# The head of a decoder trunk loaded by row group, contiguous weight chunks, and a changed TensorE ranking in the planner

## The chip, the cores and the metric

The kernel runs on one core of a Trainium2 chip (trn2). The metric is the device time of one execution in microseconds; a lower number is better. Three runs of the kernel before gave 301.43, 301.76 and 303.13 us, with a median of 301.76.

## The reference

Two layers act on x of 256 tokens by 1024 features, in float32. Each layer does the following, and a final RMSNorm comes after the second.

```python
def hybrid_layer(x, norm_w, w_in, conv_w, conv_b, gate_bias, ret_norm_w, mlstm_norm_w, w_out):
    h = rmsnorm(x, norm_w)
    proj = jnp.matmul(h, w_in)           # 1024 x 4360, all groups at once
    (aq, ak, av, ag, bq, bk, bv, bg, cq, ck, cv, co, cg, ci, cf) = jnp.split(proj, cuts, axis=-1)
    ya = moba_attention(aq, ak, av) * silu(ag)                    # 8 heads of 64, ALiBi, causal
    yb = head_norm(retention(rotate(bq), rotate(bk), bv)) * silu(bg)   # 4 heads of 64
    qk = silu(causal_dwconv(concat(cq, ck), conv_w, conv_b))
    yc = head_norm(mlstm(qk, cv, ci, cf) * sigmoid(co)) * silu(cg)     # 4 heads of 64
    return x + jnp.matmul(concat(ya, yb, yc), w_out)              # 1024 x 1024
```

At 256 tokens the attention sees one block, so it is plain causal softmax with a linear bias.

## The kernel before

**Numbers.** Each float32 operand of a projection is split into a high part (rounded to fp32r) and a low part (the rest), and a product is three matmuls: high x high, high x low, low x high. ScalarE writes the high part (`A(h, raw, Copy)`), VectorE the low part (`V("tensor_tensor", lo, raw, h, subtract)`). So every weight passes ScalarE and VectorE once.

**Chunks.** The weights of a layer lie in chunks of about 1 MB: `aq0`, `ak0`, `bq`, `bk`, `cq`, `ck`, `cvif` and so on, then four chunks of `w_out`. A chunk has 128 partitions; its columns run over 8 row groups (`k`, 128 input features each). `loader` fetches chunk after chunk into the pool `raw` (3 buffers), `splitter` writes `hi` and `lo` (3 buffers each), `project` issues the matmuls, and functions named `evac_...` take the results from PSUM and go on with attention, retention and mLSTM (`head_a`, `head_c`, `pair_a` and others).

**The head.** The first two chunks, `aq0` and `ak0`, are projected together, row group by row group: for each `k`, two chunks `z`, two column halves `t`, and three products, so 12 matmuls of 256 columns. `loader` fetches for the row groups 0, 1, 2-3, 4-5 and 6-7 one transfer of x and one of each chunk: 15 transfers. `first_x` splits x of a group (it also multiplies by the norm's weight), `first_w` the weights. In DRAM x lies as `[128, 80 + 8*256]` with the small parameters in front (`xp`), and all weights as one array `w` of `[128, 2*43072]`, so that a row of a chunk is 344,576 bytes from the next.

**Order.** One order for each engine's queue is written out beforehand by a planner, class `Sched`. Every piece of work is a generator (a thread with a priority) that yields operations with an engine and a cost in ns: `V` for VectorE, `A` for ScalarE, `G` for GpSimd, `M` and `TR` for TensorE matmuls and transposes, `D` for a DMA on SP's queue. `Sched.run` takes again and again the operation that could start first by its model (`start`, then the priority, then the age) and emits it. `LAT` (230 ns) is what it reckons for a hand-over to another engine, 1100 ns for a landing. `pause(t)` delays a thread's next operation to a time of the model; it stands before the transposes of `norm` and of `head_a`. The order is fixed once the kernel is built; at run time the engines wait for each other's semaphores only. `project` has priority 5, the attention parts 2, so these go first where both could start.

**Warm-up.** Two float32 matmuls on a zeroed tile (`dummy`, L372) precede the work on TensorE.

Almost all instructions are recorded under the lines of the helpers: L259 is `V`, L265 `A`, L280 `M`, L285 `TR`, L288 `D`. A tile's name tells more than a line: `xx` is the split x, `hi` and `lo` the split weights, `px` parameters and x, `pj` and `mx` the PSUM banks, `st`, `zu`, `zd` the split operands of the heads, `t` the pool `t512`, `et` the weights of the heads' values.

## Time and profile before

| | |
|---|---|
| Profiled execution, its time | 301.41 us |
| Its span, first to last instruction | 299.6 us |
| Median of the runs | 301.76 us |
| TensorE busy | 291.0 us, 97% |
| VectorE busy | 257.7 us, 86% |
| ScalarE busy | 196.6 us, 66% |
| GpSimd busy | 15.3 us, 5% |
| DMA | 48.58 MB, 162 GB/s over the span |
| Granted TensorE clock | 0.995 |

The profile is one execution. Busy shares are averages over very different stretches: a head in which data arrive, two layers, and an end in which the last rows are normed and written. TensorE's matmuls are pipelined: the duration of one overlaps the next, so the distance from start to start tells what a matmul costs in a stream. In a row of the timeline stand start, duration, engine, line, operation, output and input, shape, count, and in brackets the idle time before with what ended it. In a row of groups, busy time and the mean duration of one in ns follow the bar.

### The profile page before, as it was taken

How to read it: one execution, taken by the hardware profiler on the slowest of the kernel's cores; microseconds unless marked ns; L12 is line 12 of the kernel's file. 1: busy time of each engine (PE TensorE's matmuls, PEld its weight loads, DVE VectorE, ACT ScalarE, POOL GpSimd, SP SyncE). 2: the span in 40 equal slices, each digit the busy share in tenths (PEclk: the TensorE clock that was granted, in tenths of full speed). 3: DMA queues.
4: the chain of work that ended last, by engine and by line, in shares of the span. 5: the costliest groups of instructions: out<-in, count | busy, mean ns of one | idle time of the engine just before them, and what ended most of it. 6: DMA issues, size and time to landing. Idle time of an engine off the chain costs nothing.

```text
span 299.6 us, 4795 instructions
## 1 busy us (share of the span) xinstructions
PE 291.0 (97%) x1792; PEld 258.2 (86%) x1792; DVE 257.7 (86%) x549; ACT 196.6 (66%) x341; POOL 15.3 (5%) x19
## 2 busy tenths in 40 slices
PE   8899999999999999999999999999999999999991
PEld 6798989888989888899988898988899988888881
DVE  3969999999999997985679999999999999956353
ACT  5958997889448539644666699779555265845332
POOL 6000000000002002000020000000002002000010
PEclk9999999999999999999999999999999999999997
DMA  6999456574710560754317663446541624330003
GB/s 200 374 398 352 153 174 223 184 258 143 238 45 0 161 240 22 249 174 148 136 19 264 205 222 125 156 142 219 203 142 45 237 67 173 123 131 0 2 0 140
DMA packets 9095, 48.58 MB, mean 162 GB/s; under 512 B 1008, under 2 KB 1904, under 8 KB 4080
## 3 DMA queue, kind: packets, MB, share of 16 engines
q1 hardware_dynamic: 9072, 48.28, 46.7%
q8 instruction: 14, 0.23, 0.3%
q14 instruction: 9, 0.07, 0.1%
HBM read 47.23 MB, written 1.05 MB: 161 GB/s over the span
## 4 chain that ended last, share of the span: by engine, by line
PE 91%; DVE 2%; issue 2%; ACT 1%; DMA 1%; SPq 1%; POOL 0%; POOLq 0%
PE pj L280 71%; PE mx L280 15%; PE mx L285 4%; DMA px<-xp 1%; SPq L288 1%; DVE sb L259 1%; DVE t L259 1%; ACT t L265 0%; ACT hi L265 0%; POOL small L554 0%; ACT xx L265 0%; ACT raw L265 0%; POOLq L1207 0%; DVE raw L259 0%; DVE hc L259 0%
## 5 line engine op out<-in xcount | busy, mean ns | idle before, releaser
L259 DVE TENSOR_TENSOR lo<-raw,hi 128x1024 fp32r<-128x1024 f32 (+2 forms) x96 | 102.8, 1087 | 8.9 <-ACT hi L265 8.7
L265 ACT ACTIVATE hi<-raw 128x1024 fp32r<-128x1024 f32 (+2 forms) x96 | 88.8, 946 | 10.4 <-DMA raw<-w 4.6
L280 PE MATMUL pj<-hi,xx 128*128 128x512 f32 (+1 forms) x320 | 94.4, 374 | 0.0
L280 PE MATMUL pj<-xx,hi 128*128 128x512 f32 (+1 forms) x272 | 88.0, 377 | 0.7 <-ACT hi L265 0.7
L280 PE MATMUL pj<-xx,lo 128*128 128x256 f32 x240 | 68.8, 287 | 0.3 <-DVE lo L259 0.3
L280 PEld LDWEIGHTS pj<-hi,xx 128*128 128x128 f32 x320 | 57.4, 188 | 9.0
L280 PE MATMUL pj<-lo,xx 128*128 128x512 f32 (+1 forms) x160 | 59.4, 371 | 0.0
L280 PEld LDWEIGHTS pj<-xx,hi 128*128 128x128 f32 x272 | 49.9, 192 | 10.1 <-ACT hi L265 1.7
L280 PEld LDWEIGHTS pj<-xx,lo 128*128 128x128 f32 x240 | 45.8, 191 | 0.8 <-DVE lo L259 0.7
L280 PEld LDWEIGHTS pj<-lo,xx 128*128 128x128 f32 x160 | 30.1, 188 | 4.5
L265 ACT ACTIVATE sb<-sb,small 128x128 f32<-128x128 f32 (+1 forms) x48 | 19.5, 448 | 4.9 <-DVE small L259 2.4
L265 ACT ACTIVATE t<-pj 128x256 f32<-128x256 f32 x26 | 9.8, 376 | 17.0 <-PE pj L280 16.9
L265 ACT ACTIVATE st<-t 64x512 fp32r<-64x512 f32 x26 | 16.1, 627 | 4.5 <-DVE t L259 4.2
L1101 POOL TENSOR_TENSOR small<-small,mhalf 128x8 f32<-128x8 f32 x4 | 6.9, 1731 | 181.7 <-DVE small L259 181.7
L280 PE MATMUL pj<-yh,lo 128*128 128x256 f32 x56 | 15.9, 284 | 0.0
L280 PE MATMUL pj<-yh,hi 128*128 128x256 f32 x56 | 15.9, 284 | 0.0
L280 PE MATMUL pj<-yl,hi 128*128 128x256 f32 x56 | 15.8, 283 | 0.0
L280 PE MATMUL mx<-st,st 128*128 128x128 f32 (+1 forms) x64 | 15.1, 270 | 0.0
L265 ACT ACTIVATE t<-pj,small 128x512 f32<-128x512 f32 (+1 forms) x12 | 7.3, 610 | 11.2 <-PE pj L280 11.2
L259 DVE TENSOR_TENSOR t<-pj,t 128x256 f32<-128x256 f32 x26 | 10.9, 419 | 2.2 <-ACT t L265 2.1
L265 ACT ACTIVATE t<-t 32x512 f32<-32x512 f32 (+1 forms) x20 | 12.6, 629 | 0.3
L280 PEld LDWEIGHTS mx<-st,st 128*128 128x128 f32 x64 | 12.1, 189 | 0.6
(150 smaller groups left out, 480.3 us busy)
## 6 DMA issues: line engine op xcount, KB each, us to landing
raw<-w SPq DMA_DIRECT2D x37, 1024.0 KB, 4.8
raw<-w SPq DMA_DIRECT2D x2, 1056.0 KB, 6.2
raw<-w SPq DMA_DIRECT2D x6, 256.0 KB, 5.6
raw<-w SPq DMA_DIRECT2D x2, 512.0 KB, 6.8
tb<-tab SPq DMA_DIRECT2D x1, 960.0 KB, 10.0
px<-xp SPq DMA_DIRECT2D x3, 256.0 KB, 4.8
tb<-tab SPq DMA_DIRECT2D x1, 514.0 KB, 7.7
raw<-w SPq DMA_DIRECT2D x4, 128.0 KB, 2.8
```

The lines of the kernel that those rows point to most:

```text
L259: return op("dve", cost, lambda: getattr(nc.vector, name)(out, *a, **k), after)
L265: return op("act", cost, lambda: nc.scalar.activation(out, in_, func, **k), after)
L280: return op("pe", cost, lambda: nc.tensor.matmul(out, a, b, start=start, stop=stop, skip_group_check=True), after)
L285: return op("pe", 110.0, lambda: nc.tensor.transpose(out, in_, idn))
L288: return op("sp", cost, lambda: nc.sync.dma_start(out, in_))
L1101: yield G(1600, lambda: nc.gpsimd.tensor_tensor(vs, vs, mhalf[:, :8], op=OP.pow))
```

## The change

- **Head in DRAM and SBUF.** x and the first two chunks are interleaved by row group in one array `hd` and one tile `px`: for each `k` 256 columns of x, 256 of `aq0`, 256 of `ak0` (`H_K` = 768). Groups 0 and 1 come as three transfers each, groups 2 to 7 as one each: 12 transfers. Each transfer's block is contiguous in DRAM. The head no longer takes buffers of the pool `raw`.
- **Chunks.** Each later chunk is contiguous in DRAM (`block`).
- **Splitting the head.** For groups 2 to 7 both chunks are split in one step of 512 columns. The very first weight is rounded on VectorE. The first six matmuls go by product before column half, and wait for each operand by itself.
- **Buffers.** `on_a`, `on_b`, `hc` and four of the six `t512` buffers lie in places of `px` whose weights have been split.
- **Start.** Seven 128-column matmuls on a constant zero replace the two on a zeroed tile. `va`, `vc` and `cpad` are set only where nothing else writes.
- **Planner.** Matmul costs are 120.2 ns for 256 columns (before 110) and 226.8 for 512 (before 216.3). A TensorE operation that follows another engine, or has waited, is ranked as if it could start 400 ns later (`SLACK`); the time that the model then books for it is unchanged. Both `pause` calls are gone.

The diff, cut to its core:

```diff
--- before
+++ after
@@ -53,8 +53,11 @@
 W_OFFS = np.concatenate([[0], np.cumsum(W_SIZES)]).tolist()
+W_HEAD = W_OFFS[2]
 W_TOTAL = W_OFFS[-1]
+H_K = 256 + 512
@@ -114,6 +117,8 @@
+    SLACK = 400.0
     SELF = {"pe": 0.0, "dve": 130.0, "act": 130.0, "pool": 130.0, "sp": 0.0}
@@ -200,14 +205,16 @@
                         ready = max(ready, th.floor)
-                    start = max(self.free.get(eng, 0.0), ready)
+                    free = self.free.get(eng, 0.0)
+                    start = max(free, ready)
+                    by = max(free, ready + self.SLACK) if eng == "pe" and (th.src != "pe" or th.floor > th.t) else start
                     if alt is None or start + cost < alt[0]:
-                        alt = (start + cost, start, way)
+                        alt = (start + cost, start, way, by)
                 prio = th.prio() if callable(th.prio) else th.prio
-                key = (alt[1], prio, th.seq)
+                key = (alt[3], prio, th.seq)
                 if best is None or key < best[0]:
-                    best = (key, th, alt[2])
-            (start, _, _), th, (eng, cost, fn, after) = best
+                    best = (key, th, alt[2], alt[1])
+            _, th, (eng, cost, fn, after), start = best
             self.live.remove(th)
@@ -226,7 +233,7 @@
 @with_exitstack
-def trunk(ctx: ExitStack, tc: tile.TileContext, xp: bass.AP, w: bass.AP, fn: bass.AP,
+def trunk(ctx: ExitStack, tc: tile.TileContext, hd: bass.AP, w: bass.AP, fn: bass.AP,
           tab: bass.AP, out: bass.AP):
@@ -274,9 +281,9 @@
         if a.dtype == F32R:
-            cost = max(107.0, n / 2.4) + 3
+            cost = max(113.0, n / 2.4 + 13.5)
         else:
-            cost = 2 * max(107.0, n * 2 / 2.4 / 1.0) + 3
+            cost = 2 * max(108.0, n * 2 / 2.4 + 13.5)
         return op("pe", cost, lambda: nc.tensor.matmul(out, a, b, start=start, stop=stop, skip_group_check=True),
@@ -296,16 +303,11 @@
-    def pause(t):
-        ev = Event()
-        ev.time = t
-        return wait(ev)
-    px = sb_tile([128, P_N + KT * S], "px")
+    px = sb_tile([128, P_N + KT * H_K], "px")
     pr = px[:, :P_N]
-    x = px[:, P_N:].rearrange("p (k t) -> p k t", t=S)
+    hx = px[:, P_N:].rearrange("p (k c) -> p k c", c=H_K)
+    x = hx[:, :, 0:S]
     tb = sb_tile([128, T_N], "tb")
@@ -323,9 +325,9 @@
     gi = sb_tile([4, 2, S], "gi")
-    on_a = sb_tile([128, 2, 512], "on_a")
-    on_b = sb_tile([128, 2, 256], "on_b")
-    hc = sb_tile([128, 2, 256], "hc")
+    on_b, hc = [hx[:, k, 256:].rearrange("p (b c) -> p b c", b=2) for k in (4, 5)]
+    on_a = hx[:, 6:8, 256:]
     rrow = sb_tile([128, S], "rrow")
@@ -347,7 +349,7 @@
     sb_pool("lo", 3, [128, 2112], F32R)
-    sb_pool("t512", 6, [128, 512])
+    sb_pool("t512", 2, [128, 512])
     sb_pool("st", 7, [128, 512], F32R)
@@ -356,20 +358,18 @@
+    zero = nc.const_aps.tensor(0.0, (128, 128), F32)
+    for _ in range(7):
+        nc.tensor.matmul(sc.pools["mx"][0][3][0][:, :128], zero, zero, start=True, stop=True)
     nc.vector.memset(ones, 1.0)
...
     nc.vector.memset(mhalf, -0.5)
-    nc.gpsimd.memset(va, 1.0)
-    nc.gpsimd.memset(vc, 1.0)
-    nc.gpsimd.memset(cpad, 0.0)
+    nc.gpsimd.memset(va[:, :, :, HD:], 1.0)
+    nc.gpsimd.memset(vc[:, :, :, HD:], 1.0)
+    nc.gpsimd.memset(cpad[:, :, :3], 0.0)
     for tag, half in (("zu", slice(64, 128)), ("zd", slice(0, 64))):
...
             nc.gpsimd.memset(t[half].bitcast(F32), 0.0)
-    dummy = sc.pools["sb"][0][0][0]
-    nc.vector.memset(dummy, 0.0)
-    for _ in range(2):
-        nc.tensor.matmul(sc.pools["mx"][0][3][0][:, :384], dummy[:, :128], dummy, start=True, stop=True)
@@ -382,34 +382,32 @@
+    def block(a, o, n):
+        return a[o * 128:(o + n) * 128].rearrange("(p n) -> p n", n=n)
     def loader():
-        for i in range(NL):
+        for k in range(KT):
+            o = P_N + k * H_K
+            if k < 2:
+                for key, a, b in ((None, o - P_N if k == 0 else o, o + 256), (0, o + 256, o + 512), (1, o + 512, o + 768)):
+                    e = yield D((b - a) * 512 / 360.0, px[:, a:b], block(hd, a, b - a))
+                    sc.set(E("x0", k) if key is None else E("hw", k, key), e + 1100)
+                continue
+            e = yield D(H_K * 512 / 360.0, px[:, o:o + H_K], block(hd, o, H_K))
+            sc.set(E("x0", k), e + 1100)
+            for m in range(2):
+                sc.set(E("hw", k, m), e + 1100)
+        for i in range(2, NL):
             l, c = divmod(i, NW)
             n = W_SIZES[c]
-            o = l * W_TOTAL + W_OFFS[c]
-            if i == 1:
-                continue
+            o = l * W_TOTAL + W_OFFS[c] - W_HEAD
             t = yield acq("raw")
             raws[i] = t
-            if i < 2:
-                if i == 0:
-                    t1 = yield acq("raw")
-                    raws[1] = t1
-                    for a, b in ((0, 1), (1, 2), (2, 4), (4, 6), (6, 8)):
-                        o1, o2 = P_N + a * S if a else 0, P_N + b * S
-                        e = yield D((o2 - o1) * 512 / 360.0, px[:, o1:o2], xp[:, o1:o2])
-                        for k in range(a, b):
-                            sc.set(E("x0", k), e + 1100)
-                        for m in range(2):
-                            e = yield D((b - a) * 364, (t, t1)[m][:, a * 256:b * 256],
-                                        w[:, o + m * 2048 + a * 256:o + m * 2048 + b * 256])
-                            for k in range(a, b):
-                                sc.set(E("rawk", m, k), e + 1100)
-                continue
             m = 2 if i == 2 else 1
...
                 a, b = j * n // m, (j + 1) * n // m
-                e = yield D((b - a) * 512 / 360.0, t[:, a:b], w[:, o + a:o + b])
+                e = yield D((b - a) * 512 / 360.0, t[:, a:b], block(w, o, n)[:, a:b])
                 for q in range(2 * j // m, 2 * (j + 1) // m):
@@ -422,7 +420,8 @@
         wk = pr[:, P_NW + l * 8 + k:P_NW + l * 8 + k + 1]
-        yield A(xh[:, k, :], x[:, k, :], AF.Copy, scale=wk)
+        t = yield A(xh[:, k, :], x[:, k, :], AF.Copy, scale=wk)
+        sc.set(E("xh", l, k), t)
         t = yield V("scalar_tensor_tensor", xl[:, k, :], x[:, k, :], wk, xh[:, k, :].bitcast(F32),
@@ -431,12 +430,21 @@
-    def first_w(m, k):
-        yield wait(E("rawk", m, k))
-        a = slice(k * 256, (k + 1) * 256)
-        yield A(his[m][:, a], raws[m][:, a], AF.Copy)
-        t = yield V("tensor_tensor", los[m][:, a], raws[m][:, a], his[m][:, a].bitcast(F32), op=OP.subtract)
-        sc.set(E("wk", m, k), t)
+    def first_w(k, m0, m1):
+        h, lo = (t[k // 4][:, k % 4 * 512 + m0 * 256:k % 4 * 512 + m1 * 256] for t in (his, los))
+        r = hx[:, k, 256 + m0 * 256:256 + m1 * 256]
+        yield wait(E("hw", k, m1 - 1))
+        if k + m0 == 0:
+            t = yield V("tensor_copy", h, r, fast=True)
+            sc.set(E("wh"), t)
+        else:
+            yield A(h, r, AF.Copy)
+        t = yield V("tensor_tensor", lo, r, h.bitcast(F32), op=OP.subtract)
+        for m in range(m0, m1):
+            sc.set(E("wk", m, k), t)
+        if k < 4 and m1 == 2:
+            sc.release("t512", hx[:, k, 256:], t)
@@ -444,12 +452,8 @@
             sc.spawn(first_x(k), -3)
-            for m in range(2):
-                sc.spawn(first_w(m, k), -2)
-        for m in range(2):
-            for k in range(KT):
-                yield wait(E("wk", m, k))
-            sc.release("raw", raws.pop(m), E("wk", m, KT - 1).time)
+            for m0, m1 in ((0, 1), (1, 2)) if k < 2 else ((0, 2),):
+                sc.spawn(first_w(k, m0, m1), -2)
         for i in range(2, NL):
@@ -477,7 +481,7 @@
             sq = yield acq("t512")
-            yield A(sq, x[:, k:k + 2, :].rearrange("p a t -> p (a t)"), AF.Square)
+            yield A(b2(sq), x[:, k:k + 2, :], AF.Square)
             if ss is None:
@@ -493,7 +497,6 @@
         yield wait(E("tab"))
-        yield pause(e + 500)
         for b in range(2):
@@ -605,17 +608,27 @@
                             yield wait(E("w", q, 0))
-                    hv = [his[q][:, :2048].rearrange("p (k c) -> p k c", k=KT) for q in ii]
-                    lv = [los[q][:, :2048].rearrange("p (k c) -> p k c", k=KT) for q in ii]
+                    if i:
+                        hv, lv = [[t[q][:, :2048].rearrange("p (k c) -> p k c", k=KT) for q in ii] for t in (his, los)]
+                    else:
+                        hv, lv = [[[t[k // 4][:, (k % 4 * 2 + z) * 256:(k % 4 * 2 + z + 1) * 256] for k in range(KT)]
+                                   for z in range(m)] for t in (his, los)]
                     for k in range(KT):
-                        yield wait(E("x", l, k))
+                        yield wait(E("xh" if i + k == 0 else "x", l, k))
                         for z in range(m):
-                            yield wait(E("wk", z, k) if i == 0 else E("w", i + z, k // 4))
-                            for t in range(2):
-                                cs = slice(t * 128, (t + 1) * 128)
-                                for q, (a, b) in enumerate(((hv[z], xh), (hv[z], xl), (lv[z], xh))):
-                                    e = yield M(ps[z][:, t * 256:(t + 1) * 256], a[:, k, cs], b[:, k, :],
-                                                k + t + q == 0, k == KT - 1 and q == 2)
+                            ak = [v[z][:, k] if i else v[z][k] for v in (hv, lv)]
+                            qt = [(q, t) for t in range(2) for q in range(3)]
+                            if i + k + z == 0:
+                                yield wait(E("wh"))
+                                qt.sort()
+                            else:
+                                yield wait(E("wk", z, k) if i == 0 else E("w", i + z, k // 4))
+                            for q, t in qt:
+                                a, b = ((ak[0], xh), (ak[0], xl), (ak[1], xh))[q]
+                                if i + k + z == 0 and q:
+                                    yield wait(E("x", l, k) if q == 1 else E("wk", z, k))
+                                e = yield M(ps[z][:, t * 256:(t + 1) * 256], a[:, t * 128:(t + 1) * 128], b[:, k, :],
+                                            k + t + q == 0, k == KT - 1 and q == 2)
                     for z, q in enumerate(ii):
@@ -869,7 +882,6 @@
         pt = yield acq("mx")
-        yield pause(e + 400)
         for j in range(3):
@@ -1181,7 +1193,7 @@
     x, w_in, w_out = f(x), f(w_in), f(w_out)
-    xT = x[0].T.reshape(KT, 128, S).transpose(1, 0, 2).reshape(128, KT * S)
+    xT = x[0].T.reshape(KT, 128, S).transpose(1, 0, 2)
     w = np.empty((128, DEPTH * W_TOTAL), np.float32)
@@ -1199,7 +1211,12 @@
     fn = np.ascontiguousarray(np.broadcast_to(f(final_norm_w), (128, D_)))
-    ins = {"xp": np.concatenate([par, xT], 1), "w": w, "fn": fn, "tab": _tables()}
+    head = np.concatenate([xT, w[:, :2048].reshape(128, KT, 256), w[:, 2048:W_HEAD].reshape(128, KT, 256)], 2)
+    head = np.concatenate([par, head.reshape(128, -1)], 1)
+    cuts = [P_N + k * H_K + c for k in range(KT) for c in ((0, 256, 512) if k < 2 else (0,))][1:]
+    blocks = lambda a, cuts: np.concatenate([b.reshape(-1) for b in np.split(a, cuts, axis=1)])
+    ends = [l * W_TOTAL + o - W_HEAD for l in range(DEPTH) for o in W_OFFS[1:]]
+    ins = {"hd": blocks(head, cuts), "w": blocks(w[:, W_HEAD:], ends[2:-1]), "fn": fn, "tab": _tables()}
```

## The prediction

> **What bounds the kernel now.** I read the page first (engine shares, slices, chain), then windows of the head and of the rest, then the timeline of the first 12 us.
>
> ```profile
> span 299.6 us, 4795 instructions
> PE 291.0 (97%) x1792; PEld 258.2 (86%) x1792; DVE 257.7 (86%) x549; ACT 196.6 (66%) x341; POOL 15.3 (5%) x19
> PE 91%; DVE 2%; issue 2%; ACT 1%; DMA 1%; SPq 1%; POOL 0%; POOLq 0%
> ...
> 3.90:18.56 14.66, 13.62 (x97) 12.90 (x97) 12.57 (x29) 11.97 (x28) 1.19 (x3) 1.00 0.99 348
> 18.57:293.27 274.70, 274.51 (x1693) 244.03 (x1692) 242.45 (x513) 180.97 (x306) 10.16 (x7) 1.00 0.45 154
> 161.00:257.00 96.00, 95.81 (x569) 83.95 (x568) 93.97 (x208) 66.03 (x110) 3.64 (x2) 1.00 0.48 165
> ```
>
> The last three rows are stretches: length, busy time of PE, PEld, DVE, ACT, POOL with counts, clock, DMA share, GB/s. The reader sees a TensorE queue that is full for 274.51 of 274.70 us once the first block is through. What remains to be won lies before 18.57 us, and after 293.27 in a tail that the change does not touch. In the second layer VectorE is as full as TensorE (93.97 of 96.00 us), so there is hardly a reserve there.
>
> The first block (weight chunks aq0 and ak0) is 8 row groups of 12 matmuls, 96 in all; it starts at 3.92 us and hands over at 18.57, so it takes 14.65 us.
>
> ```profile
> 0.73 0.38 SPq L288 DMA_DIRECT2D px<-xp  x1
> 3.53 0.43 SPq L288 DMA_DIRECT2D px<-xp  x1
> 1.37 2.93 PE L372 MATMUL mx<-sb 128*128 128x384 f32 x4 [1.37 <-DVE sb L370]
> 3.05 0.51 ACT L265 ACTIVATE xx<-px 128x256 fp32r<-128x256 f32 x1 [0.83 <-DMA px<-xp]
> 3.92 0.81 PE L280 MATMUL pj<-xx,hi 128*128 128x256 f32 x2
> 5.28 0.41 PE L280 MATMUL pj<-xx,lo 128*128 128x256 f32 x1
> 5.49 0.63 PE L280 MATMUL pj<-xx,hi 128*128 128x256 f32 x2
> 6.48 0.42 ACT L265 ACTIVATE hi<-raw 128x256 fp32r<-128x256 f32 x1 [0.26 <-DMA raw<-w]
> 7.63 0.91 ACT L265 ACTIVATE xx<-px 128x256 fp32r<-128x256 f32 x2 [0.73 <-DMA px<-xp]
> 7.88 0.29 PE L280 MATMUL pj<-xx,lo 128*128 128x256 f32 x1
> 8.90 0.50 PE L280 MATMUL pj<-xx,hi 128*128 128x256 f32 x2 [0.73 <-ACT hi L265]
> 10.79 0.38 PE L280 MATMUL pj<-xx,lo 128*128 128x256 f32 x1 [0.26 <-DVE lo L259]
> 11.37 0.40 PE L280 MATMUL pj<-xx,hi 128*128 128x256 f32 x2
> 11.61 0.28 PE L280 MATMUL pj<-xx,lo 128*128 128x256 f32 x1
> ```
>
> Starts are the thing to read here. At 5.28 to 5.49 one matmul takes 0.21 us (cold clock); at 11.37 to 11.61 two take 0.24, so 0.12 each. At 0.12 the 96 would take 11.52 us: the block loses 3.1 us. Of this about 1.1 lies before the clock rises (6.1 us), 0.9 in the hole between 7.88 and 8.90, and 1.0 in holes up to 10.79. The holes come from data: row groups 2 and 3 arrive as a pair, their x at 7.63, then pass ScalarE and VectorE.
>
> **The change, part by part.**
>
> *Head transfers.* Same bytes, 3.19 MB. Before: 15 transfers in rows of 1 and 2 KB. After: six for groups 0 and 1 (rows of 1 KB, as before), then one of 0.39 MB (rows of 3 KB) for each group. SP's issues come at the same times up to 3.53 us, when group 2 goes out; then three issues fewer, so 1.4 us of SP (three times its 0.48 us step), which hides under the transfers. Which arrival binds? Groups 0 and 1 are split 0.83 MB into the stream and reach their last split at 6.48; group 2 ends at 1.22 MB, where before group pair 2/3 had its x at 1.09 MB. The prices of transfer and split:
>
> ```profile
> 2.00:7.50 5.50, 5.50 (x25) 4.21 (x23) 2.49 (x6) 3.16 (x9) 3.03 (x6) 1.00 0.91 267
> 12.50:20.00 7.50, 7.50 (x61) 7.32 (x61) 6.82 (x14) 4.96 (x10) 0.00 (x0) 1.00 1.02 398
> 18.60:24.60 6.00, 6.00 (x39) 5.33 (x38) 3.25 (x7) 2.40 (x3) 0.71 (x1) 1.00 1.01 423
> L265 ACT ACTIVATE xx<-px 128x256 fp32r<-128x256 f32 x8 | 3.7, 503 | 1.6 <-DMA px<-xp 1.6
> L265 ACT ACTIVATE t<-px 128x512 f32<-128x512 f32 x4 | 2.5, 616 | 0.0
> L259 DVE SCALAR_TENSOR_TENSOR xx<-px,xx 128x256 fp32r<-128x256 f32 x8 | 3.6, 483 | 3.1 <-ACT xx L265 3.1
> L259 DVE TENSOR_TENSOR t<-t,t 128x512 f32<-128x512 f32 x3 | 2.1, 686 | 0.0
> L259 DVE TENSOR_TENSOR lo<-raw,hi 128x256 fp32r<-128x256 f32 x16 | 6.1, 420 | 1.2 <-ACT hi L265 1.2
> L259 DVE TENSOR_TENSOR lo<-raw,hi 128x1024 fp32r<-128x1024 f32 x2 | 2.4, 1222 | 0.0
> ```
>
> The DMA engines are 91% busy at only 267 GB/s while rows of 1 and 2 KB run, and move 398 GB/s with mixed, longer rows. From landing to a ready group: ScalarE 0.50 for x, 0.62 for both weights in one 512-wide step (priced by the 512-wide square), VectorE 0.69 for the low half (priced by the 512-wide add): 1.81, with hand-overs 1.85 us. TensorE then has six groups left, 72 x 0.12 = 8.64. Later groups follow each other by 0.39 MB / 398 GB/s = 0.99 us, less than the 1.44 that TensorE needs, so group 2 alone decides; VectorE's 0.48 + 0.69 + half an add of 0.69 is 1.52 a group, which could give back up to 6 x 0.08 = 0.5 if the norm's adds are not put off.
> Bounds for group 2: at the old rate, 0.13 MB behind the 7.63 row, 7.63 + 0.13/0.267 = 8.1, and the block ends at 18.6: gain 0. At 398 GB/s after 6.48: 7.47, end 17.96: gain 0.6. Held up by the issue alone: the first transfer took 0.73 to 3.05, so 2.3 us for 0.17 MB; 3.53 + 2.3 + 0.22/0.398 = 6.4, ready at 8.25, end 16.9: gain 1.7. I take 0.6, nearest to the row in which 4 KB rows ran.
>
> *Contiguous chunks.* Past the head nothing waits for a slow transfer: rows of 8 KB at the old pitch already ran at 423 GB/s (window 18.60 to 24.60). 0.
> The Trainium skill, "DMA: Bandwidth & Descriptors", section "Latency and other measured facts", says that a row pitch at a large power of two halves a load's rate and that contiguous tiles restore it. The pitch here is 2 x 43,072 x 4 = 344,576 bytes, no such power, so by that rule the new layout brings nothing, as the 423 GB/s agrees; only longer rows are left.
>
> *Warm-up.* The new zero matmuls need no VectorE memset; TensorE can start near 0.8 rather than 1.37. Before, a 384-column pass stepped 0.64 (2.93 for four with the last one's tail), so 14 passes of 128 columns take 14 x 0.21 = 3.0 and end by 3.9, when data come. An earlier rise of the clock shortens groups 0 and 1 only, and TensorE then waits for group 2: 0 with the middle arrival, up to 0.5 with the early one. The same cover takes the VectorE copy of the first weight and the sorted first six matmuls: 0. The smaller POOL memsets cost nothing; POOL's first consumer comes at 21.5.
>
> *Raw buffers.* Head data no longer sit in the pool, so chunks 2, 3 and 4 are issued at once. That removes ScalarE's longest wait, in which TensorE did not wait: 0, but it gives VectorE room to follow a block that ends earlier.
>
> ```profile
> ACT hi L265 <- DMA raw<-w: 4.6, 3, 3.7
> L494 POOL TENSOR_TENSOR small<-small,mhalf 128x2 f32<-128x2 f32 x2 | 2.3, 1156 | 54.9 <-DVE small L259 54.9
> 256.11 0.27 PE L285 MATMUL mx<-tb,t 128*128 128x128 f32 x1
> 256.56 0.31 PEld L285 LDWEIGHTS mx<-tb,t 128*128 128x128 f32 x3 [0.54 <-DVE t L259]
> 20.69 0.50 PE L280 MATMUL mx<-ones,t 128*128 128x1 f32 x4
> 21.05 0.48 PE L280 MATMUL pj<-xx,hi 128*128 128x512 f32 x1
> 21.37 0.28 PE L280 MATMUL pj<-xx,lo 128*128 128x256 f32 x1
> 21.48 0.40 PE L280 MATMUL pj<-xx,hi 128*128 128x512 f32 x1
> 21.72 0.28 PE L280 MATMUL pj<-xx,lo 128*128 128x256 f32 x1
> ```
>
> *Scheduler.* The new costs (120.2 and 226.8 ns) are what the trace steps: 0.12, and 0.24 at 21.48. SLACK ranks a TensorE operation 400 ns later if it follows another engine. It replaces the two pauses: the norm's pow is costed 630 but takes 1156, late by 0.53; if nothing else is ready, its transposes stall TensorE up to 0.5 twice. The one late operand in the middle is at 256.11: 0.45 to the next start. SLACK or the new order may save about 0.35 there; I take it. A switch from the f32 matmuls to the split ones costs TensorE 0.09 (21.05 to 21.37 is 0.32, 21.48 to 21.72 is 0.24); regrouped attention work may have ten more or ten fewer switches: 0, range +-0.9.
>
> *Buffers moved into px* (on_a, on_b, hc, four of six t512): same instructions. If ordering is tracked more coarsely there, one 0.69 VectorE step per layer border might wait: 0 to 1.4, taken 0 since the buffers are used between borders.
>
> **Sum.** 0.62 + 0.35 = 0.97. The profiled execution took 301.41 us; 301.41 - 0.97 = 300.4. The median of the runs shown is 301.76, 0.1% above it.
>
> **Rivals.**
> A. *Transfers stay as slow.* For: the engines were already 91% busy at 267 GB/s, and groups 0 and 1 keep 1 KB rows. Group 2 lands at 8.1 and only 0.35 is left: 301.1. Chance 0.22. (By the rule on row pitch in the Trainium skill, "DMA: Bandwidth & Descriptors", section "Latency and other measured facts", it comes out this way.)
> B. *The middle arrival*, the forecast, 300.4. Chance 0.36.
> C. *Arrival held by the issue alone.* For: contiguous blocks and 3 KB rows; against: the first six transfers are as small as before. Gain 1.7 plus 0.35: 299.4. Chance 0.30.
> The Trainium skill, "TensorE: Matmul & The Clock Gate", Part 1, has the clock rise after a busy window of about 3.4 us whose phase is free. The rise at 6.1 after the first matmul at 1.37 agrees; by it the earlier start may bring the rise 0.6 forward on average, 0.3 us of matmuls, and only where data are there (case C).
> D. *Slower: the attention chains come late.* Each hand-over back to TensorE may now lie 0.4 us longer; a head has three in a row (scores, transposes, values), 1.2 us, at the end of each layer. At 256.11 TensorE already ran out of other ready work once, so there the delay goes into the time. It decides once project's matmuls of a layer are used up before its last head. Twice 1.2, less 0.6 of the head: 301.41 + 1.8 = 303.2. Against: SLACK only ranks, and work was ready for 274.51 of 274.70 us. Chance 0.12.
>
> **How the numbers follow.** About 0.5% (1.5 us) can be told from no change. Against 301.76, faster is below 300.25: nearly all of C (0.29), not quite half of B (0.16), 0.01 of A: 0.46. Slower, above 303.27: 0.11 for most of D with a few mishaps of A. Within: 0.43. Signs of both sides hold chances, so B's own range, from the switches and VectorE's adds, is 299.6 to 301.2. The range 298.7 to 302.4 takes in C with a warm start (299.4 less 0.5 and noise) and A with ten more switches, and leaves out most of D.
>
> **What would show it.** In the timeline, group 2 (the 25th split matmul) starting near 9.3 shows B, near 10 A, near 8.3 C; the block's hand-over near 17.9 the same. GB/s of 2 to 7.5 us against 267 shows whether the layout quickens transfers. After that, TensorE busy in all but 0.2 us up to its last matmul shows that the shift survives; holes at 120 to 130 or 250 to 260 released by VectorE show D. The prediction is wrong if the rest of the run changes its length by more than the head does.

## The result and the profile after

The changed kernel is slower: 306.08 us (median of 4 runs, 305.76 to 306.67) against 301.60 for the kernel before on the same chip (4 runs, 300.63 to 303.13). The ratio is 1.0146, 95% interval 1.0127 to 1.0164. Forecast were 300.4 us and a range of 298.7 to 302.4. The profiled execution took 306.08 us. One run of e9 below (742.03 us) and three of the kernel before (323.85, 742.93 and 1020.27) lie far off all the others and are left out of medians and ratios.

In the kernel after, the helpers' lines are L266 (VectorE, `V`), L272 (ScalarE, `A`), L287 (`M`), L292 (`TR`), and the head's data are called `px<-hd`. Its page has these rows for span, busy time and the shares of the chain that ended last:

```profile
span 304.3 us, 4794 instructions
...
PE 293.7 (97%) x1802; PEld 259.7 (85%) x1802; DVE 257.6 (85%) x542; ACT 196.3 (65%) x335; POOL 14.7 (5%) x19
...
PE 45%; DVE 35%; ACT 11%; issue 4%; DMA 2%; POOL 1%; SPq 1%; POOLq 0%; DVEq 0%; ACTq 0%
```

The engines do the same work (VectorE 257.6 us, before 257.7). What changed is the chain: before, 91% of it was TensorE's own queue; now VectorE and ScalarE hold 46%. The share is not a length of waiting: wherever TensorE waits for a result, the chain passes over to the engine that made it and runs back along that engine's queue. In the windows below TensorE's idle time past the first block is 2.2 us, before 0.2; the rest of what it lost lies inside durations and shows only from start to start. The windows of the kernel after tell where (columns as in the prediction: length, busy PE, PEld, DVE, ACT, POOL, clock, DMA share, GB/s):

```profile
2.00:7.50 5.50, 5.50 (x30) 5.28 (x29) 2.59 (x7) 2.84 (x8) 0.98 (x2) 1.00 0.89 270
3.79:18.72 14.93, 13.60 (x98) 12.82 (x98) 11.97 (x24) 11.30 (x22) 0.00 (x0) 1.00 1.00 361
...
18.73:297.73 279.00, 276.79 (x1693) 243.79 (x1692) 243.19 (x511) 181.68 (x307) 11.67 (x7) 1.00 0.42 150
161.00:257.00 96.00, 94.97 (x565) 82.97 (x564) 91.09 (x188) 63.70 (x104) 5.15 (x2) 1.00 0.45 159
```

The head did not get shorter (hand-over of the first block at 18.73 us, before 18.57). From there to the start of the last matmul TensorE issues the same 1693 instructions in 279.00 us instead of 274.70: +4.30 us, nearly the whole loss. I call this length **the rest** below. It is the measure for the planner's order, since the head's own scatter is not in it.

TensorE's groups name the work that lost most of it: the transposes of the softmax weights in `head_a` (`mx<-tb,sb`). First the weight load's group before, then after (busy and mean of one, then idle time before them):

```profile
L285 PEld LDWEIGHTS mx<-tb,sb 128*128 128x128 f32 x48 | 6.0, 142 | 1.2
```
```profile
L292 PEld LDWEIGHTS mx<-tb,sb 128*128 128x128 f32 x48 | 5.6, 141 | 4.6 <-ACT sb L272 3.7
```

The idle time before these 48 loads grew by 3.4 us, and ScalarE's `sb` releases most of it, the Exp of the softmax. Two of the places in the timeline of the kernel after:

```profile
51.08 0.41 DVE L266 CUSTOM_DVE_ANT_0 sb<-mx,tb 128x256 f32<-128x256 f32 x1
51.20 1.20 ACT L272 ACTIVATE sb<-sb,small 128x128 f32<-128x128 f32 x3 [0.43 <-DVE small L266]
51.31 0.27 PE L292 MATMUL mx<-tb,sb 128*128 128x128 f32 x1
51.42 0.08 DVE L266 DVE_READ_ACCUMULATOR2_ANT small<- 128x1 f32 x1
...
52.05 0.73 PE L292 MATMUL mx<-tb,sb 128*128 128x128 f32 x4 [0.48 <-ACT sb L272]
...
186.26 1.09 ACT L272 ACTIVATE hi<-raw 128x1056 fp32r<-128x1056 f32 x1
...
186.88 0.27 PE L292 MATMUL mx<-tb,sb 128*128 128x128 f32 x1
187.25 0.49 ACT L272 ACTIVATE sb<-sb,small 128x256 f32<-128x256 f32 x1
...
187.79 0.44 PE L292 MATMUL mx<-tb,sb 128*128 128x128 f32 x2 [0.65 <-ACT sb L272]
```

A head's first transpose goes out at 186.88, but the Exp for the second stands on ScalarE behind the split of a whole weight chunk and starts at 187.25. The next entry of TensorE's queue needs that Exp: from 186.88 to 187.79 nothing else is issued, 0.91 us where one transpose follows another after 0.11 (rows of f1 below). The same from 51.31 to 52.05, where the Exp itself waits for VectorE's bias-and-max (the operation that adds the bias to the scores and takes their maximum). The transposes stand a little too early in a fixed order. Start to start, TensorE has nine holes that are 0.1 to 0.8 us longer than the usual distance, 3.6 us together. Four of them, 2.3 us, stand before these transposes and are released by ScalarE. The other five, 1.3 us, stand before other work; VectorE releases four of them, GpSimd one (0.13 us before the norm's transposes, at 158.21).

Of the head, three moments (ScalarE taking row group 2, and TensorE around it):

```profile
8.11 0.28 PE L287 MATMUL pj<-xx,lo 128*128 128x256 f32 x1
8.42 0.51 ACT L272 ACTIVATE xx<-px 128x256 fp32r<-128x256 f32 x1 [1.28 <-DMA px<-hd]
...
9.50 0.51 PE L287 MATMUL pj<-xx,hi 128*128 128x256 f32 x2 [1.11 <-ACT hi L272]
...
18.73 0.40 PE L287 MATMUL pj<-xx,hi 128*128 128x512 f32 x1
```

Group 2 landed at 8.4 us, later than both the forecast's 7.47 and the 8.1 of rival A, and 2.00 to 7.50 moved 270 GB/s against 267. The trace has sixteen semaphore updates for group 2's transfer: fifteen have come by 7.70 us, the last comes at 8.40, and ScalarE starts at 8.42.

### The profile page after: what moved, and what is told of

The parts are those of the page before. It is cut to its first block, busy times and chain, and to the rows that moved or that the text cites. A ratio compares the mean times of both kernels' runs of the same rounds, so it can differ in the third digit from the quotient of the medians.

```text
span 304.3 us, 4794 instructions
## 1 busy us (share of the span) xinstructions
PE 293.7 (97%) x1802; PEld 259.7 (85%) x1802; DVE 257.6 (85%) x542; ACT 196.3 (65%) x335; POOL 14.7 (5%) x19
## 4 chain that ended last, share of the span: by engine, by line
PE 45%; DVE 35%; ACT 11%; issue 4%; DMA 2%; POOL 1%; SPq 1%; POOLq 0%; DVEq 0%; ACTq 0%
PE pj L287 34%; DVE lo L266 12%; PE mx L287 8%; DVE px L266 6%; DVE small L266 4%; ACT hi L272 4%; DVE st L266 3%; PE mx L292 3%; DVE sb L266 3%; ACT px L272 2%; ACT sb L272 2%; DVE t L266 2%; DMA px<-hd 2%; DVE et L266 1%; ACT st L272 1%
## 5 line engine op out<-in xcount | busy, mean ns | idle before, releaser
L266 DVE TENSOR_TENSOR lo<-raw,hi 128x1024 fp32r<-128x1024 f32 (+1 forms) x80 | 96.7, 1218 | 6.5 <-ACT hi L272 6.3
L287 PE MATMUL pj<-hi,xx 128*128 128x512 f32 (+1 forms) x320 | 93.8, 373 | 0.0
L272 ACT ACTIVATE hi<-raw 128x1024 fp32r<-128x1024 f32 (+1 forms) x80 | 83.1, 1056 | 12.5 <-issue 5.6
L287 PE MATMUL pj<-xx,hi 128*128 128x512 f32 (+1 forms) x272 | 87.6, 377 | 1.1 <-ACT hi L272 1.1
L287 PE MATMUL pj<-xx,lo 128*128 128x256 f32 x240 | 68.4, 286 | 0.2 <-DVE lo L266 0.2
L287 PEld LDWEIGHTS pj<-hi,xx 128*128 128x128 f32 x320 | 57.4, 188 | 9.1 <-DVE px L266 0.2
L287 PE MATMUL pj<-lo,xx 128*128 128x512 f32 (+1 forms) x160 | 60.0, 375 | 0.0
L287 PEld LDWEIGHTS pj<-xx,hi 128*128 128x128 f32 x272 | 49.8, 193 | 9.8 <-ACT hi L272 1.5
L287 PEld LDWEIGHTS pj<-xx,lo 128*128 128x128 f32 x240 | 45.7, 191 | 0.7 <-DVE lo L266 0.6
L287 PEld LDWEIGHTS pj<-lo,xx 128*128 128x128 f32 x160 | 30.1, 188 | 4.4
L272 ACT ACTIVATE sb<-sb,small 128x128 f32<-128x128 f32 (+1 forms) x48 | 19.1, 447 | 13.8 <-DVE small L266 10.3
L272 ACT ACTIVATE st<-px 64x512 fp32r<-64x512 f32 x24 | 14.9, 631 | 8.3 <-DVE px L266 7.1
L1113 POOL TENSOR_TENSOR small<-small,mhalf 128x8 f32<-128x8 f32 x4 | 8.4, 2109 | 183.9 <-DVE small L266 183.9
L287 PE MATMUL pj<-yh,lo 128*128 128x256 f32 x56 | 15.9, 284 | 0.0
L287 PE MATMUL pj<-yh,hi 128*128 128x256 f32 x56 | 15.9, 284 | 0.0
L287 PE MATMUL pj<-yl,hi 128*128 128x256 f32 x56 | 15.8, 283 | 0.0
L287 PE MATMUL mx<-st,st 128*128 128x128 f32 (+1 forms) x64 | 15.1, 269 | 0.1
L287 PEld LDWEIGHTS mx<-st,st 128*128 128x128 f32 x64 | 12.1, 189 | 1.0 <-DVE px L266 0.4
L287 PEld LDWEIGHTS mx<-va,et 128*128 128x128 f32 x96 | 11.6, 192 | 0.3
L287 PE MATMUL pj<-hi,yh 128*128 128x512 f32 (+1 forms) x32 | 11.8, 369 | 0.0
L287 PE MATMUL pj<-hi,yl 128*128 128x512 f32 (+1 forms) x32 | 11.8, 368 | 0.0
L287 PE MATMUL pj<-lo,yh 128*128 128x512 f32 (+1 forms) x32 | 11.7, 366 | 0.0
```

The source lines that it names most:

```text
L266: return op("dve", cost, lambda: getattr(nc.vector, name)(out, *a, **k), after)
L272: return op("act", cost, lambda: nc.scalar.activation(out, in_, func, **k), after)
L287: return op("pe", cost, lambda: nc.tensor.matmul(out, a, b, start=start, stop=stop, skip_group_check=True), after)
L1113: yield G(1600, lambda: nc.gpsimd.tensor_tensor(vs, vs, mhalf[:, :8], op=OP.pow))
```

## The experiments

Unless said otherwise a median is of 4 runs, the ratio is to the kernel before on the same chip, and the rest is read from the window of each kernel's profile as above.

| kernel | us | ratio, 95% interval | rest, us |
|---|---|---|---|
| after | 306.08 | 1.0146 [1.0127, 1.0164] | 279.00 |
| e1 (10 runs) | 302.93 | 1.0039 [1.0010, 1.0068] | 275.35 |
| e2 | 306.74 | 1.0174 [1.0120, 1.0228] | 278.94 |
| e3 | 309.68 | 1.0254 [1.0211, 1.0298] | 281.52 |
| e4 (10 runs) | 303.37 | 1.0055 [1.0021, 1.0089] | 276.26 |
| e5 | 305.02 | 1.0122 [1.0078, 1.0165] | 277.99 |
| e6 | 307.59 | 1.0191 [1.0163, 1.0218] | 281.30 |
| e7 | 306.59 | 1.0160 [1.0131, 1.0189] | 280.50 |
| e8 (10 runs) | 300.34 | 0.9962 [0.9942, 0.9983] | 274.72 |
| e9 (3 runs) | 303.44 | 1.0062 [1.0042, 1.0081] | 277.42 |
| e10 | 309.38 | 1.0265 [1.0233, 1.0298] | 282.76 |
| e11 | 305.18 | 1.0112 [1.0095, 1.0129] | 278.60 |
| e12 | 307.59 | 1.0199 [1.0174, 1.0224] | 279.61 |
| f1 | 303.58 | 1.0073 [1.0056, 1.0090] | 277.76 |
| f2 | 299.70 | 0.9944 [0.9929, 0.9958] | 274.25 |
| f3 (10 runs) | 301.11 | 0.9985 [0.9971, 0.9999] | 274.68 |
| f4 | 302.88 | 1.0057 [1.0039, 1.0074] | 277.01 |
| g1 | 306.32 | 1.0150 [1.0114, 1.0185] | 280.65 |
| g2 (10 runs) | 301.61 | 0.9981 [0.9957, 1.0005] | 274.87 |

**Which of the planner's three edits?** Each is undone by itself in the kernel after (e1 the matmul costs, e2 the pauses, e3 SLACK), then all three (e4).

```diff
e1: -            cost = max(113.0, n / 2.4 + 13.5)
    +            cost = max(107.0, n / 2.4) + 3
    -            cost = 2 * max(108.0, n * 2 / 2.4 + 13.5)
    +            cost = 2 * max(107.0, n * 2 / 2.4 / 1.0) + 3
e2: +        yield pause(e + 500)          # in norm, ahead of its transposes
    +        yield pause(e + 400)          # in head_a, ahead of its transposes
e3: -    SLACK = 400.0
    +    SLACK = 0.0
e4: e1 + e2 + e3
```

> The changed kernel with the old matmul costs in the planner (110 and 216.3 ns), everything else as changed. Theory 1 (the true costs take away a reserve: as long as the planner thought TensorE 5% faster than it is, every hand-over had time in hand): most of the 4.3 us comes back, 301.5 to 302.5. Theory 2 (the two pauses are what is missed): still near 305, with the waits of the transposes mx<-tb,sb for ScalarE as in the changed kernel, 3 us. Theory 3 (the 400 ns ranking costs it): still near 305. Theory 4 (the buffers in px, the layout): still near 306.

> The changed kernel with both pauses put back (400 ns before the transposes of head_a, 500 before those of norm), new costs and the ranking kept. Theory 2: the 3.1 us that the transposes mx<-tb,sb gained go, 302.5 to 303. Theory 1: the ranking already books these transposes later than a pause of 400 would, so little changes, 305 to 306. Theories 3 and 4: 305 to 306.

> The changed kernel with the 400 ns ranking set to 0, new costs, no pauses. Theory 3: back to 302 to 303. Theories 1 and 2: nothing now keeps a distance to ScalarE, so more waits, 307 to 310. Theory 4: 306.

> The changed kernel with the whole old planner: old costs, both pauses, no ranking; so head, layout, buffers and warm-up are changed alone. Theories 1, 2 and 3: as before, 301 to 302 (the first block handed over at 18.73 against 18.57 us, so no gain from the head). Theory 4: still 304 to 306, with waits on px.

Rival D, as the prediction had it, falls: without SLACK the kernel is slower still (309.68), so SLACK wins time here, 3.6 us, of which 2.5 in the rest. The pauses win nothing: the waits for the Exp shrink (the idle time before the transposes' loads goes from 4.6 to 2.4 us), and others take their place. The old matmul costs alone bring the rest from 279.00 to 275.35, and TensorE's idle time in it from 2.2 to 0.9 us; e1's window:

```profile
19.05:294.40 275.35, 274.43 (x1693) 244.30 (x1692) 246.00 (x516) 178.53 (x302) 9.38 (x7) 1.00 0.42 152
```

The costs were the edit that the prediction had priced at nothing.

**The same from the other side.** The kernel before, with nothing but the new matmul costs (e6), and with the whole new planner (e7: costs, SLACK, no pauses).

```diff
e6: kernel before
    -            cost = max(107.0, n / 2.4) + 3
    +            cost = max(113.0, n / 2.4 + 13.5)
    -            cost = 2 * max(107.0, n * 2 / 2.4 / 1.0) + 3
    +            cost = 2 * max(108.0, n * 2 / 2.4 + 13.5)
e7: e6, SLACK = 400.0 with its ranking, both pause calls out
```

> The kernel before with nothing changed but the planner's matmul costs (120.2 and 226.8 ns; both pauses kept, no ranking). Theory 1: slower than before by 3 to 6 us, 304 to 308, with waits of TensorE for VectorE and ScalarE in the heads. If the loss needs the new head, layout or buffers too: 301.5 to 302.5.

> The kernel before with the whole new planner (new costs, ranking, no pauses) and the old head, layout and buffers. Theory 1: 304 to 306, about what the changed kernel takes. If the head and the buffers cost about 1.3 us by themselves, as the run with the old planner on the changed kernel says: 304.5, so that much below the changed kernel.

Four constants make the kernel before 6 us slower, with no transfer and no buffer changed. Window and group of e6 (there `TR` is L285, ScalarE L265):

```profile
18.21:299.51 281.30, 276.56 (x1693) 243.57 (x1692) 242.98 (x510) 182.66 (x309) 11.62 (x7) 1.00 0.44 151
L285 PEld LDWEIGHTS mx<-tb,sb 128*128 128x128 f32 x48 | 5.5, 143 | 5.6 <-ACT sb L265 4.8
```

Compare the 274.70 and 1.2 of before: the same hole at the same transposes. So the loss does not need the new head, layout or shared buffers.

**The head by itself.** e8 has the old planner of e4, and groups 0 and 1 also come as one transfer each, in rows of 3 KB, split in one 512-column step as the others are.

```diff
-            if k < 2:
+            if False:
                 for key, a, b in ((None, ...
-            e = yield D(H_K * 512 / 360.0, px[:, o:o + H_K], block(hd, o, H_K))
+            a = o if k else 0
+            e = yield D((o + H_K - a) * 512 / 360.0, px[:, a:o + H_K], block(hd, a, o + H_K - a))
-            for m0, m1 in ((0, 1), (1, 2)) if k < 2 else ((0, 2),):
+            for m0, m1 in ((0, 2),):
```

> The changed kernel with the old planner, and groups 0 and 1 fetched in one transfer each like groups 2 to 7 (rows of 3 KB; group 0 carries the parameters), split in one step of 512 columns. If the first six transfers with rows of 1 KB hold the stream up: groups land about 1.0 us apart from 3.6 us on, the hole before group 2 goes, and the first block hands over near 17 us where it was 18.88; the time falls by 1 to 1.8 us against that run, 301.5 to 302.5. If the DMA engines' own rate binds from the start: group 2 lands near 8 us again and the block hands over at 18.5 or later, because group 0 starts later; 303 to 304.

```profile
2.00:7.50 5.50, 4.51 (x26) 3.82 (x25) 2.69 (x5) 2.50 (x7) 0.98 (x2) 1.00 0.97 312
17.59:292.31 274.72, 274.54 (x1694) 244.09 (x1692) 243.03 (x514) 181.24 (x306) 11.23 (x7) 1.00 0.43 153
```

312 GB/s in the stretch that had 267 and 270, the hand-over at 17.59, and a rest of 274.72 against 274.70. In e8 group 2 reaches ScalarE at 7.28 us instead of 8.42. This is the gain that the prediction had looked for, in the place where it was looked for: the six transfers in rows of 1 KB stood in its way. (e8 changes the number of transfers, the length of their rows and the splits behind them together; which of these counts was not separated.) (Over all profiles, the seven with the change's head hand over at 18.37 to 19.21 us, mean 18.8, the ten with e8's at 16.95 to 18.96, mean 18.0; the last section says what scatters them.) In the equal rest there is no sign that contiguous chunks, raw buffers and the buffers inside `px` cost or bring anything, but the scatter of the orders below is too large to call it shown. e8 is faster than both kernels, by 0.4% against the one before.

**Why do truer costs give a slower order?** One theory: the costs of the other engines are too low in the model as well, and the errors cancelled. e5 corrects those that stood out in the trace (bias-and-max, GpSimd's powers). Another: high TensorE costs leave the chains no reserve. e12 books the 400 ns instead of only ranking by them.

```diff
e5: -            cost = n / 1.3                      # bias-and-max
    +            cost = n / 0.96 + 76
    -        G(630, ...), G(1600, ...), G(500, ...)
    +        G(1160, ...), G(1730, ...), G(800, ...)
e12: -  start = max(free, ready); by = max(free, ready + self.SLACK) if ... else start
     +  if eng == "pe" and (th.src != "pe" or th.floor > th.t): ready += self.SLACK
     +  start = by = max(free, ready)
```

> The changed kernel, with new matmul costs and ranking, and now also with the costs of the other engines that the trace of before gives: VectorE's bias-and-max (tensor_tensor_reduce) 210 and 343 ns for 128 and 256 columns where the planner has 98 and 197, GpSimd's pow 1160, 1730 and 800 where it has 630, 1600 and 500. Theory 1a (the true TensorE costs hurt because the other costs stayed too low, 257 ns of VectorE a head, 4.1 us over 16 heads): 302 to 303. Theory 1b (any planner that reckons TensorE at its true speed loses the distance between its order and the run, whatever the rest): 305 to 306.

> The changed kernel with true costs, where the 400 ns are booked and not only ranked: in the planner a TensorE operation that follows another engine, or has waited, cannot start earlier than 400 ns after it is ready. Theory 1b as a matter of distance in time: the waits go, 302 to 303.5. If it is not the distance at a hand-over but what the planner takes for the scarce engine (with the true costs it takes TensorE for the slowest, and puts the heads' work for VectorE later): 304.5 to 307.

In e5 the rest is 1 us shorter, which is less than the scatter of the orders below and so not shown as a gain; booking (e12) wins nothing. Then the costs in steps, all on e8: matmul costs x 1.025 (e9), x 0.95 (e10); and e8's head and costs with SLACK and without pauses (e11).

> The version with one transfer a group and the old planner (it ran 300.34), with all matmul costs of the planner raised by 2.5%, half of the way to the true ones. Theory 1b (what counts is how far the planner reckons TensorE faster than it runs): between, 302 to 303.5, with some waits of TensorE for the heads. Rival (an order is good or bad by chance, the costs only reshuffle it): anywhere from 299.5 to 306, no sequence.

> The same version with all matmul costs lowered by 5% against the old ones, so about 10% under the true ones. Theory 1b: the distance is larger than needed; no waits of TensorE, 299.5 to 301 as at the old costs, or a little more if work of the heads is put in too early for a full VectorE. Rival of chance: anywhere from 299.5 to 306.

> One transfer a group, old matmul costs, the 400 ns ranking on, no pauses. If ranking helps at the old costs too: 299 to 300.3. If it is needed only where the distance is gone: 300 to 301, as with the old planner.

Upwards it goes as the theory has it: 300.34, 303.44, and 306 to 310 at the true costs. But x 0.95 loses most of all in the rest (282.76), by another kind of wait. The two longest in the waits of e10:

```profile
PEld pj L287 <- DVE lo L266: 2.7, 3, 2.1
PEld mx L292 <- DVE px L266: 2.5, 2, 2.3
```

TensorE runs dry of prepared operands: weights not yet split (37 us), outputs of layer 1 not yet ready (125 us). e11 loses time at 125 to 129 us as well, for VectorE's results. SLACK in place of the pauses has thus no fixed price at the old costs: with the head of the change the times are 302.93 with it (e1) and 303.37 without (e4), with e8's head 305.18 (e11) and 300.34 (e8).

That leaves two readings: the old costs lie at a balance, or any change of a constant draws another order and the old ones drew a lucky one. Four more kernels, all on e8, with two partners in the end:

```diff
f1: matmul costs x 1.005      f2: matmul costs x 0.995      f4: LAT = 234.0 (was 230.0)
f3: new matmul costs; every other cost (V, A, G, D, TR, LAT, SELF) x 1.06
g1: new matmul costs; nothing else        g2: as f3, x 1.065
```

> Every matmul cost x 1.005 on e8_one_transfer (old costs, pauses, no SLACK, one transfer per group, 300.34 us). Theory 'chance' (a static order falls well or badly, and e8 and the kernel before are good draws): half a per cent already gives another order, so the time lies anywhere from 300 to 306, and one of this run, f2 and f4 is over 302.5. Theory 'balance' (the time follows the ratio of the model's TensorE costs to the others smoothly, with a flat minimum at the old costs): 300.0 to 301.2, in line with 303.7 at 1.025. Theory 'higher TensorE costs always lose' (linear from 300.34 at 1 to 303.7 at 1.025): 301.0.

> Every matmul cost x 0.995 on e8_one_transfer. Chance: 300 to 306, see f1. Balance: 300 to 301.5 (309.4 at 0.95 by the other kind of wait, for VectorE at the end of layer 1). Linear in the cost: 299.7.

> e8_one_transfer with LAT 234 instead of 230, a change of 4 ns that says nothing on any engine's speed; it makes another order all the same. Chance: anywhere from 300 to 306. Balance or any theory in which the costs' sizes decide: 300.0 to 301.0.

> e8_one_transfer with the true matmul costs, and every other cost of the model (VectorE, ScalarE, GpSimd, DMA, transposes, LAT, SELF) x 1.06, so that the ratio of TensorE (mean of the two matmul costs, weighted by their counts: +6.25%) to the rest is about that of the old costs. If only the ratio counts: 300 to 301.5, and the true costs were harmful because the other costs stayed too low beside them. If true matmul costs harm by themselves: 305 to 307. If it is chance: anywhere from 300 to 308, and it then stays open.

> e8_one_transfer with the true matmul costs and every other cost as it was: the partner of f3 (301.11), which differs only in the factor 1.06 on the other costs. If the ratio is what hurts: 305 to 308, about the 307.6 of e6 less 1.3 for the head. If f3 and e6 were only different draws of the order, it lies anywhere from 300 to 307, and under 303 would speak against the ratio.

> f3 with the factor 1.065 instead of 1.06: a second order at nearly the same ratio. If the ratio of the costs decides, with a scatter of some 2 us as f1, f2 and f4 showed at the old ratio: 299.5 to 304. If f3 was a lucky draw among orders planned with true matmul costs: 305 to 309.

Both hold, and the runs tell their sizes. *Chance:* half a per cent up costs 3.2 us, half a per cent down wins 0.6 (0.5 in the rest), 4 ns in a constant cost 2.5. Without SLACK and at the old ratio of costs the rests are 274.70 (before), 276.26 (e4), 274.72 (e8), 277.76 (f1), 274.25 (f2) and 277.01 (f4): mean 275.8, spread 3.5. f1 and f4 lose most of theirs near 126 us. The stretch 125 to 130 us before, then the same of f1 with its timeline:

```profile
125.00:130.00 5.00, 5.00 (x40) 4.86 (x39) 4.30 (x6) 3.29 (x5) 0.00 (x0) 1.00 0.51 195
```

```profile
125.00:130.00 5.00, 3.81 (x25) 2.88 (x24) 4.26 (x12) 4.40 (x8) 0.00 (x0) 1.00 0.50 200
...
125.50 0.27 PE L292 MATMUL mx<-tb,t 128*128 128x128 f32 x1
125.61 0.27 PE L292 MATMUL mx<-tb,px 128*128 128x128 f32 x1
126.17 0.33 PE L292 MATMUL mx<-tb,t 128*128 128x128 f32 x1 [0.29 <-DVE t L266]
...
126.47 0.36 PE L287 MATMUL pj<-yh,hi 128*128 128x256 f32 x1
127.16 0.39 PE L287 MATMUL pj<-yl,hi 128*128 128x256 f32 x1 [0.33 <-DVE yl L266]
```

Before, TensorE is busy for all 5.00 us of that stretch; here it is for 3.81, because the last outputs of layer 1 come late. *The ratio:* with the new matmul costs beside unscaled others, and without SLACK, the rests are 281.52 (e3), 281.30 (e6) and 280.65 (g1): mean 281.2, 5.4 above the other mean, and the lowest of the three still lies 2.9 above the highest of the six. With the same true matmul costs and the others raised alike they are 274.68 (f3) and 274.87 (g2). Windows and groups of f3, then of g1:

```profile
18.30:292.98 274.68, 274.52 (x1693) 244.43 (x1692) 242.59 (x512) 181.40 (x307) 10.66 (x7) 1.00 0.42 152
L292 PEld LDWEIGHTS mx<-tb,sb 128*128 128x128 f32 x48 | 6.0, 141 | 1.8 <-ACT sb L272 0.4
```
```profile
17.75:298.40 280.65, 276.89 (x1693) 243.87 (x1692) 243.70 (x512) 182.34 (x308) 11.61 (x7) 1.00 0.41 149
L292 PEld LDWEIGHTS mx<-tb,sb 128*128 128x128 f32 x48 | 5.4, 143 | 4.5 <-ACT sb L272 3.9
```

The two differ by a factor of 1.06 on the costs of everything but the matmuls, and the wait for the Exp (3.9 us) is there in the one and all but gone (0.4) in the other. So the cause is the ratio of the model's costs, about 5.4 us, of which SLACK hides perhaps 2 in the change (after, e2, e5, e7 and e12, which have it beside the new costs, lie at 277.99 to 280.50, mean 279.2; with the scatter of the orders that is a rough figure). What stays open is which of the other costs are too low: e5 raised two kinds, and its 1 us does not stand out of the scatter.

## Why the prediction was wrong, point by point

- **The failed step is the one on the planner**: "The new costs ... are what the trace steps", and no price behind it. True, and beside the point. A planner's cost isn't paid in the time; it sets how far ahead of their operands instructions are placed, relative to all other costs. It should have been a term with both signs and, by e6, up to 6 us: the largest of the change. Taking the costs alone back returns 3.65 of the 4.30 us (e1).
- **"SLACK or the new order may save about 0.35"**: its effect depends on the rest of the model: 2.5 us of the rest won at the new costs (e3), 3.9 lost at the old ones with e8's head (e11, in which the pauses are out as well), and no more than the scatter of the orders between e1 and e4.
- **The pauses**: "if nothing else is ready, its transposes stall TensorE up to 0.5 twice". The norm's transposes stalled TensorE once, by 0.13 us. Larger holes, 0.35 to 0.81, stand before `head_a`'s transposes, whose pause went too, but restoring both pauses (e2, 306.74) doesn't help.
- **Rival D** had the right side, and holes in the heads, as expected. Its agent was wrong (the costs, not SLACK), its price of 1.8 too low, and of the 3.6 us in holes ScalarE releases 2.3, VectorE, which it named, 1.2.
- **The argument against D**, "work was ready for 274.51 of 274.70 us", is the deeper error, and it misled the whole forecast: this row shows that one order had no holes, and says nothing on how near it was to having them. A row that could have warned is VectorE at 93.97 of 96.00 us in the second layer; it was read as "hardly a reserve", and not priced for a re-planned order. The prediction's own last sign of being wrong came in: the rest changed by 4.30 us, the head by 0.16.
- **Head transfers**: forecast -0.62 us, measured +0.16 at the hand-over. Rival A's mechanism was right, with 270 GB/s; group 2's first matmul starts at 9.50 us, between the marks for B (9.3) and A (10). The Trainium skill, "DMA: Bandwidth & Descriptors", section "Latency and other measured facts", reports lower rates for row pitches at large powers of two. That was measured on copies between tensors in device memory; that contiguity alone brings nothing at a pitch of 344,576 bytes is the prediction's inference from it. The trace agrees with the inference. The lever lay in e8's edit: fewer and larger transfers, with their splits joined.
- **Contiguous chunks, raw buffers, shared buffers, warm-up at 0**: nothing contradicts it; e8's rest (274.72 against 274.70) gives no sign of a cost or a gain of the first three, within the scatter of the orders. After the warm-up the first split matmul starts at 3.79 us, before at 3.92.

## What to carry to other kernels

Where a static planner writes the order, an edit of its costs is an edit of every instruction's place: price it by running that edit alone, and keep the costs in proportion to each other before making any of them true. A full queue in the profile is no sign of slack; half a per cent on the matmul costs moved this kernel by 3 us, so a planner's edit is judged by several neighbouring constants, not by one. For a head that waits on data, put together small transfers first; here that won 0.8 us of the hand-over on average: 1.3 in the six profiles whose matmuls reached their short step early, nothing in the other four (last section).

## What the runs showed of the hardware

The change from the long to the short matmul step, which the prediction calls the clock's rise, has two places for one and the same head. The warm-up matmuls run from 0.77 to 4.1 us in all kernels with e8's head; of their profiles, e8 has its 256-column matmuls at 0.12 us each from 5.76 on, while f1 steps 0.21 until 9.66. The clock column does not show it: it reads 1.00 in the kernel after for 2.00 to 7.50 us, though the split matmuls step 0.21 there until 5.85. Two matmuls, then the start of the next row, e8 first:

```profile
6.00 0.40 PE L287 MATMUL pj<-xx,hi 128*128 128x256 f32 x2
6.23 0.28 PE L287 MATMUL pj<-xx,lo 128*128 128x256 f32 x1
```
```profile
8.38 0.63 PE L287 MATMUL pj<-xx,hi 128*128 128x256 f32 x2
8.81 0.41 PE L287 MATMUL pj<-xx,lo 128*128 128x256 f32 x1
```

The hand-over lies at 17.59 us in the one and at 18.78 in the other. Of the ten profiles with e8's head, six have at most two long split matmuls (0.41 us or more in the trace, where short ones in a stream last 0.28) and hand over at 16.95 to 17.86, mean 17.55; four (e11, f1, f3, g2) have long ones until 8.6 to 10.1 us and hand over at 18.30 to 18.96, mean 18.75. With the change's head the last long one starts by 6.41 us in all seven profiles, and their mean is 18.8. So in the four late profiles e8's head won nothing. The ten runs of e8 fall into two groups, 299.88 to 300.36 and 301.25 to 301.57, about as far apart as the hand-overs. The profiled run of e8 (300.36, early) lies in the lower group; that of g2 (301.88, late) lies with the upper runs of g2 (301.35 to 301.95), whose lower ones took 300.38 to 300.59. That the step explains both groups is likely, and not shown, since only one run of each kernel has a profile. It is why the rest, and not the time alone, was compared above. The Trainium skill, "TensorE: Matmul & The Clock Gate", Part 1, says that the window behind the rise runs freely, so that the same kernel has varying numbers of cold matmuls. The traces agree as far as different kernels with one head can: none of e8's split matmuls is long, and 22 of f1's are.
